# Front of a hybrid attention/recurrence block: the second pair's projection steps set among its transposes, value weights cast earlier, one remainder on GpSimd

## The chip, the cores and the metric

One core of a Trainium2 chip. The metric is the device time of one execution in microseconds; the kernel before takes 1420.89 us in the median of 3 runs (1420.53 to 1420.9). Five engines work beside each other, each with its own queue in a fixed order: PE (TensorE, matrix products into PSUM), DVE (VectorE), ACT (ScalarE), POOL (GpSimd) and SP (SyncE, which issues most transfers).

## The reference, cut to what matters

```
xn = rmsnorm(x, norm1_g)                       # x: 1024 tokens x 1024, fp32
u  = xn @ w_in                                 # all projections
q_sb, k_sb, v_sb, f_raw, i_hg, q_hg, g_hg, gate_sb, gate_hg = split(u)
o_sb = stick_breaking_attention(q_sb, k_sb, v_sb)      # 8 heads of 64
o_hg = hgrn2(...)                                      # 4 heads of 128, gated recurrence
merged = sigmoid(gate_sb) * (o_sb @ w_o_sb) + sigmoid(gate_hg) * (o_hg @ w_o_hg)
h = x + merged @ w_out
h = h + square(relu(rmsnorm(h) @ w_ff1)) @ w_ff2
return rmsnorm(h, final_g)
```

Only the front is touched: the first normalisation, and the projection to the values `v_sb` and to the query and key of head 0.

## The kernel before

Every fp32 operand of a product is written as a rounded high part and a remainder, `h` and `l`. A product `x @ w` is then three matmuls: `xh·wh + xl·wh + xh·wl` (`three`, and `v_part` for the values). The high part is a copy on ACT (`hi_copy`, line 156: a CAST in the profile), the remainder a subtraction on DVE (`lo_sub`, line 161).

The 1024 tokens are 8 blocks of 128, `xt[0..7]`; the profile calls them all x. A block is normalised in this way: half of its squares are summed on ACT, half on DVE (line 281), the two sums are added, GpSimd takes the inverse root (`inv_root`, line 274, the tile n_y), and DVE multiplies the block by it (line 664, the scaling). Blocks 0 and 1 are the first pair, 2 and 3 the second; blocks 4 to 7 follow with their sums wholly on ACT (line 295).

`norm_transpose` turns normalised blocks so that features lie on the partitions: PE transposes 128x128 pieces into a PSUM bank (xnt, line 131), ACT writes the high part xnh (line 348) and DVE the remainder xnl (line 351), which reads the bank and xnh. For a pair there are 8 such banks (one for each of 8 feature slices `kt`), two transposes each. PSUM has 8 banks in all; the running sums of the query/key projection (pjqk) and of two value blocks (two banks pjv) hold three while the second pair is turned.

The value weights come in four tiles, wvr in the profile, split into wvh and wvl (`Unit.split`, the unit is named "wv"). Each tile holds two slices `kt`: tile 0 serves `kt` 0 and 1, tile 1 serves 2 and 3, tile 2 serves 4 and 5 (the third weights) and tile 3 serves 6 and 7 (the fourth).

The first job (`first_job`) is a generator of steps. Each call `st.advance(n, 1)` puts the next `n` steps into PE's queue; their order there is the order of the code. The steps are: four of the query/key projection for the first pair; products of blocks 0 and 1 with the high parts of value tiles 0 and 1; products with their remainders (the last part of these, `kt` 2 and 3, uses the remainder of tile 1); four query/key steps for the second pair; then the value products with tiles 2 and 3, and the rest.

Between `turns["on"] = True` and `False`, ACT and DVE execute their instructions in the order in which the code issues them (`in_turn`). An instruction on GpSimd is not held by that. `owed_wlo` keeps remainders that are to be subtracted later, and `lo_now` issues them.

Of the kernel before, what the change touches and what calls it, by code (L numbers as in the profile page):

```python
# [9 lines left out]
F32 = mybir.dt.float32  # L10
# [4 lines left out]
ALU = mybir.AluOpType  # L15
# [24 lines left out]
def kernel(  # L40
# [19 lines left out]
    nc = tc.nc  # L60
# [14 lines left out]
    def slot(name, dt=F32):  # L75
        return spool.tile([P, 1024], dt, tag="s", name=name)
# [7 lines left out]
    def bank(name):  # L84
        return psum.tile([P, 512], F32, tag="p", name=name)
# [19 lines left out]
    def after(ins, earlier):  # L105
        if earlier is not None and earlier.ins is not ins.ins:
            tc.add_manual_dep(ins.ins, earlier.ins.name, NOSYNC, reason="issue order")
        return ins

    def open_block(name):  # L110
        cur[0] = name
        lane = lanes[name]
        lane.gates = (lane.last,)
        if name == "main":
            lane.ends.append(lane.last)
        else:
            ends = lanes["main"].ends
            lane.gates += tuple(ends[-AHEAD : len(ends) - AHEAD + 1])
# [8 lines left out]
    def matmul(*a, **k):  # L127
        return pe(nc.tensor.matmul(*a, **k))  # L128

    def transpose(dst, src):  # L130
        return pe(nc.tensor.transpose(dst, src, ident))  # L131
# [9 lines left out]
    def lo_now(behind=None):  # L141
        while owed_wlo:
            after(owed_wlo.pop()(), behind)
# [3 lines left out]
    def in_turn(engine, ins):  # L147
        if turns["on"]:
            after(ins, turns[engine])
            turns[engine] = ins  # L150
        return ins
# [3 lines left out]
    def hi_copy(dst, src):  # L155
        hi_last[0] = after(in_turn("act", nc.scalar.copy(dst, src)), hi_behind[0])  # L156

    def lo_sub(dst, src, hi):
        return in_turn(
            "dve",  # L160
            nc.vector.tensor_tensor(out=dst, in0=src, in1=hi.bitcast(F32), op=ALU.subtract),  # L161
        )

    def hi_lo(h, l, src):
        hi_copy(h, src)
        return lo_sub(l, src, h)
# [29 lines left out]
    expo = cpool.tile([P, NT], F32, tag="expo", name="expo")  # L196
# [74 lines left out]

    def inv_root(mean, name):
        y = small.tile([P, 1], F32, tag="rs_y1", name=f"{name}_y", bufs=4)
        nc.gpsimd.tensor_tensor(out=y, in0=mean, in1=expo[:, 0:1], op=ALU.pow)
        return y

    def mean_square(scr, src, before, name):
# [7 lines left out]
        )  # L285
        return out

    last_power = [None]

    last_evac = [None]  # L290

# [27 lines left out]
            c = (kt % 2) * 512 + (tb % 4) * P  # L319
            return h[:, c : c + P], l[:, c : c + P]  # L320

    def norm_transpose(acts, half, b0, n, between=None):

        banks = {}

        def turn_block(kt, b):
            if kt not in banks:
                banks[kt] = bank(f"xnt{half}{kt}_{b0}")[:, 0 : n * P]
            open_block("main")
            transpose(  # L330
                banks[kt][:, b * P : (b + 1) * P],
                xt[4 * half + b0 + b][:, kt * P : (kt + 1) * P],
            )

        ahead = 6 if between else 0
        for kt in range(ahead):
            turn_block(kt, 0)
        if between:
            between()
        for kt in range(KT):  # L340
            hi, lo = acts.t.get((half, kt // 2)) or acts.make(half, kt // 2)
            cs = slice(kt % 2 * 512 + b0 * P, kt % 2 * 512 + (b0 + n) * P)
            for b in range(n):
                if b > 0 or kt >= ahead:
                    turn_block(kt, b)
            pb = banks[kt]
            g = prm[:, G1 + kt : G1 + kt + 1]
            in_turn("act", nc.scalar.activation(hi[:, cs], pb, AF.Identity, scale=g))
            in_turn(
                "dve",  # L350
                nc.vector.scalar_tensor_tensor(
                    out=lo[:, cs],
                    in0=pb,
                    scalar=g,
                    in1=hi[:, cs].bitcast(F32),
                    op0=ALU.mult,
                    op1=ALU.subtract,
                ),
            )

    class Quads:

# [33 lines left out]
        def split(self, i, kp, src, pr=0, n=4):  # L396
            if (i, kp) not in self.hl:
                self.hl[i, kp] = tuple(slot(f"sq{n_}{i}{kp}", F32R) for n_ in "hl")
            h, l = (self.part(t, pr, n) for t in self.hl[i, kp])
            self.last_lo = hi_lo(h, l, self.part(src, pr, n))  # L400
# [44 lines left out]
    class Unit:  # L445
# [28 lines left out]
        def split(self, upto=None):  # L474
            self.load(upto)
            self.hl = self.hl or []
            for i, r in list(enumerate(self.raw))[len(self.hl) : upto]:
                if self.wide:
                    h = slot(f"{self.name}h{i}", F32R)
                    l = slot(f"{self.name}l{i}", F32R)  # L480
                else:
                    h = wpool.tile([P, 1024], F32R, tag="whi", name=f"{self.name}h{i}")
                    l = wpool.tile([P, 1024], F32R, tag="wlo", name=f"{self.name}l{i}")
                self.hl.append((h, l))
                if self.name == "wf1" or self.name == "wv" and i == 1:
                    hi_copy(h, r)
                    owed_wlo.append(lambda h=h, l=l, r=r: lo_sub(l, r, h))
                    continue
                after(after(hi_lo(h, l, r), last_lo[0]), attended[0])

# [73 lines left out]
    st = Stream()  # L564
# [42 lines left out]
    def wide_unit(name, mat, c0, n):  # L607
        rows = 1024 // n * P
        return Unit(
            name,  # L610
            [
                [(0, n, mat[r : r + rows, c0 : c0 + n].rearrange("(k p) c -> p k c", p=P))]
                for r in range(0, D, rows)
            ],
            wide=True,
        )


    xn = Acts("xn")
# [77 lines left out]
    def qk_item(h):  # L697
        u = cols_unit(f"wqk{h}", [(W_IN, C_Q + h * DHS, DHS), (W_IN, C_K + h * DHS, DHS)])
        return f"pjqk{h}", u, qk_epilogue(h)
# [24 lines left out]
    def first_job():  # L724
        name, u_qk, ep = qk_item(0)
        u_qk.__class__ = FirstUnit
        u_v = wide_unit("wv", W_IN, C_V, 512)
        u_v.roomy = range(4)
        open_banks = {}

        def v_part(tb, kt, hi=True, lo=True):
            if kt == 0 and hi:
                open_banks[tb] = bank(f"pjv_{tb}")
            ps = open_banks[tb]
            sh, sl = xn.stat(kt, tb)
            wh, wl = (w[:, kt % 2 * 512 : (kt % 2 + 1) * 512] for w in u_v.hl[kt // 2])
            if hi:
                matmul(ps, sh, wh, start=kt == 0, stop=False)
                matmul(ps, sl, wh, start=False, stop=False)
            if lo:  # L740
                matmul(ps, sh, wl, start=False, stop=kt == KT - 1)

        def v_steps(tb, kts):
            for kt in kts:
                v_part(tb, kt)
                if kt == KT - 1:
                    v_epilogue(open_banks.pop(tb), tb)
                if kt % 2 == 1:
                    yield

        def qk_steps(ps, half, b0, n):
            ts = slice(b0 * P, (b0 + n) * P)
            return proj_half(ps[:, ts], u_qk.hl[0], xn.mov, KT, half, ts=ts)

        def body():
            ps = bank(f"{name}_0")
            yield from qk_steps(ps, 0, 0, 2)
            for hi in (True, False):
                for k0 in (0, 2):
                    for tb in range(2):  # L760
                        for kt in (k0, k0 + 1):
                            v_part(tb, kt, hi, not hi)
                    yield
            yield from qk_steps(ps, 0, 2, 2)
            ep(ps, 0)
            st.prefetch()
            for tb in range(4):
                yield from v_steps(tb, range(4, KT) if tb < 2 else range(KT))
            ps = bank(f"{name}_1")
            yield from qk_steps(ps, 1, 0, 4)  # L770
            ep(ps, 1)
            for tb in range(4, NT):
                yield from v_steps(tb, range(KT))

        return st.add([u_qk], body), u_qk, u_v

    j_first, u_qk0, u_v = first_job()
    j_qk = {0: j_first}

# [1554 lines left out]
    u_v.split(2)  # L2334
    norm1((2, 3), half_means((2, 3)))
    lo_now()
    st.advance(3, 1)
    norm_transpose(xn, 0, 2, 2)
    u_v.split()
    st.advance(5, 1)  # L2340
    norm1(range(4, NT))
    st.advance(8, 1)
    norm_transpose(xn, 1, 0, 4)
# [16 lines left out]
    for i, it in enumerate(items):  # L2360
# [12 lines left out]
        def between():  # L2373
            if before:
                values(*before)

        r = turn(*it, between)
# [135 lines left out]
```

## Time and profile before

| | |
|---|---|
| median of 3 runs | 1420.89 us (1420.53 to 1420.9) |
| the profiled execution | 1421.05 us, span 1419.3 us |
| granted TensorE clock, mean | 0.999 |
| PE busy | 1409.0 us |
| DVE busy | 1087.3 us |
| ACT busy | 684.4 us |
| POOL busy | 147.9 us |

The span is the time from the first to the last instruction in the profile; the execution is some 1.75 us longer. A timeline row has the start and the duration in us, the engine, the line, the operation, the tile written and the tiles read, shapes, and how many alike were put together; in brackets stands how long the engine idled before it and what released it. Instructions of one engine overlap a little in these rows, because the next one starts while the last one drains: the spacing of starts is then the better measure. A matmul row of 0.28 us can stand every 0.12 us.

### The profile page before, as it was taken

The numbers are of one execution on the slowest core, as the hardware profiler recorded it, in microseconds if no ns is written. First come the engines' busy times: TensorE is split into PE (matmuls) and PEld (weight loads), VectorE is DVE, ScalarE is ACT, GpSimd is POOL, SyncE is SP. The second block draws the span as 40 slices with busy tenths as digits, with TensorE's granted clock in tenths as the row PEclk, the third lists the DMA queues.
The fourth block names the chain that finished last, engine by engine and source line by source line (L and its number), as shares of the span: only waits on it lengthen the run. The fifth ranks groups of instructions, "written<-read, shape, count | busy, mean of one in ns | idle before, by whom it ended". The sixth has DMA issues, their size and how long they took to land.

```text
span 1419.3 us, 18799 instructions
## 1 busy us (share of the span) xinstructions
PE 1409.0 (99%) x6848; PEld 1183.7 (83%) x6848; DVE 1087.3 (77%) x1494; ACT 684.4 (48%) x1181; POOL 147.9 (10%) x341
## 2 busy tenths in 40 slices
PE   9999999999999999999999999999999999999997
PEld 8888888888888888888888888888888888888886
DVE  7579988988567888887788897676666657768765
ACT  6356676664243554433344764445444443433343
POOL 3012223210011031000000300000000000000042
PEclk9999999999999999999999999999999999999999
DMA  7024445535135685364585514444446974776825
GB/s 243 26 67 127 106 99 98 107 77 155 60 74 174 221 223 182 123 213 156 163 297 193 185 58 166 163 163 145 140 141 242 355 259 154 275 278 239 275 98 179
DMA packets 163173, 237.72 MB, mean 167 GB/s; under 512 B 26332, under 2 KB 93448, under 8 KB 163080
## 3 DMA queue, kind: packets, MB, share of 16 engines
q1 hardware_dynamic: 146056, 190.37, 40.0%
q0 software_dynamic: 11584, 34.61, 10.0%
q10 hardware_dynamic: 5440, 11.54, 2.3%
q8 instruction: 54, 0.88, 0.2%
q14 instruction: 39, 0.32, 0.1%
HBM read 168.32 MB, written 66.06 MB: 165 GB/s over the span
## 4 chain that ended last, share of the span: by engine, by line
PE 98%; DVE 1%; ACT 1%; POOL 0%; DMA 0%; issue 0%; SPq 0%; DVEq 0%; ACTq 0%
PE pm L128 21%; PE pX L128 9%; PE pW L128 6%; PE pY L128 6%; PE pjqk L128 6%; PE pga L128 4%; PE gX L128 4%; PE gY L128 4%; PE pjf L128 3%; PE pjq L128 3%; PE pys L128 3%; PE pji L128 3%; PE pyh L128 3%; PE pjv L128 3%; PE po L128 3%; PE z L128 2%
## 5 line engine op out<-in xcount | busy, mean ns | idle before, releaser
L156 ACT CAST whid<-w 128x1024 fp32r<-128x1024 f32 x30 | 31.6, 1053 | 154.5 <-PE pm L128 89.8
L826 DVE TENSOR_TENSOR_SCAN rm<-rm,bits 128x511 f32<-128x511 f32 (+7 forms) x72 | 87.3, 1219 | 17.2 <-ACT rm L804 17.1
L128 PE MATMUL pm<-wlod,sh 128*128 128x512 f32 x240 | 93.5, 390 | 0.0
L128 PE MATMUL pm<-whid,sl 128*128 128x512 f32 x240 | 93.4, 389 | 0.0
L128 PE MATMUL pm<-whid,sh 128*128 128x512 f32 x240 | 93.4, 389 | 0.0
L128 PE MATMUL pm<-tl,sh 128*128 128x512 f32 (+1 forms) x210 | 81.3, 387 | 0.0
L128 PE MATMUL pm<-th,sl 128*128 128x512 f32 (+1 forms) x210 | 81.3, 387 | 0.0
L128 PE MATMUL pm<-th,sh 128*128 128x512 f32 (+1 forms) x210 | 81.3, 387 | 0.0
L161 DVE TENSOR_TENSOR wlod<-w,whid 128x1024 fp32r<-128x1024 f32 x30 | 36.7, 1222 | 55.2 <-ACT whid L156 55.1
L161 DVE TENSOR_TENSOR sl<-sa,sh 128x1024 fp32r<-128x1024 f32 x56 | 68.2, 1218 | 0.0
L156 ACT CAST wTh<-pw 128x512 fp32r<-128x512 f32 (+2 forms) x96 | 43.8, 485 | 41.9 <-PE pw L131 41.0
L2141 POOL TENSOR_SCALAR fss<-fss 128x1 f32<-128x1 f32 x8 | 4.5, 561 | 562.0 <-ACT fsc L2136 561.5
L156 ACT CAST sh<-sa 128x1024 fp32r<-128x1024 f32 x56 | 57.2, 1046 | 7.0 <-DMA sa<-ad 7.0
L128 PEld LDWEIGHTS pm<-wlod,sh 128*128 128x128 f32 x240 | 45.0, 187 | 9.9 <-DVE wlod L161 0.4
L128 PEld LDWEIGHTS pm<-whid,sh 128*128 128x128 f32 x240 | 45.1, 188 | 9.4
L161 DVE TENSOR_TENSOR wTl<-pw,wTh 128x512 fp32r<-128x512 f32 (+2 forms) x96 | 49.9, 546 | 3.9 <-ACT wTh L156 3.7
L128 PEld LDWEIGHTS pm<-whid,sl 128*128 128x128 f32 x240 | 45.1, 188 | 9.3
L169 DVE TENSOR_TENSOR bt<-bt,rm 128x511 f32<-128x511 f32 (+7 forms) x72 | 48.9, 684 | 3.5
L804 ACT ACTIVATE rm<-z 128x511 f32<-128x511 f32 (+4 forms) x96 | 48.0, 500 | 5.5 <-PE z L128 2.9
L128 PE MATMUL pX<-sql,t1h 128*128 128x512 f32 x128 | 49.9, 390 | 0.0
L128 PE MATMUL pX<-sqh,t1l 128*128 128x512 f32 x128 | 49.9, 390 | 0.0
L128 PE MATMUL pX<-sqh,t1h 128*128 128x512 f32 x128 | 49.8, 389 | 0.0
(930 smaller groups left out, 4435.9 us busy)
## 6 DMA issues: line engine op xcount, KB each, us to landing
w<-in_w_ff_dram SPq DMA_DIRECT2D x72, 512.0 KB, 4.8
sa<-ad SPq DMA_DIRECT2D x52, 512.0 KB, 6.4
ad<-a SPq DMA_DIRECT2D x32, 256.0 KB, 4.6
ad<-s SPq DMA_DIRECT2D x16, 512.0 KB, 3.3
tw<-in_w_out_dram POOLq DMA_DIRECT2D x24, 256.0 KB, 4.6
pr<-pd SPq DMA_DIRECT2D x10, 512.0 KB, 6.5
x<-in_x_dram SPq DMA_DIRECT2D x8, 512.0 KB, 7.8
xnl<-xnh POOLq DMA_DIRECT2D x8, 512.0 KB, 6.4
```

Of the source, the lines that this page charges most:

```text
L128: return pe(nc.tensor.matmul(*a, **k))
L156: hi_last[0] = after(in_turn("act", nc.scalar.copy(dst, src)), hi_behind[0])
L161: nc.vector.tensor_tensor(out=dst, in0=src, in1=hi.bitcast(F32), op=ALU.subtract),
L169: return nc.vector.tensor_tensor(out=out, in0=a, in1=b, op=ALU.mult)
L804: nc.scalar.activation(rm[:, s0 + c0 - 1 : s0 + m - 1], z[:, c0:m], AF.Sigmoid, scale=-0.125)
L826: sc = nc.vector.tensor_tensor_scan(out=rr, data0=rr, data1=bits[:, 1024 - nk + a : 1024 - nk + b][:, ::-1], initial=rm[:, b : b + 1] if i ...
L2141: nc.gpsimd.tensor_scalar(out=ssq, in0=ssq, scalar1=1.0 / D, scalar2=EPS, op0=ALU.mult, op1=ALU.add)
```

## The change

The projection steps of the second pair are no longer put behind its transposes but among them: `norm_transpose` gets an argument `then`, called after each slice `kt`, and three query/key steps are issued after slices 4, 6 and 7. In the generator, the last part of the remainder products of value tiles 0 and 1 moves behind the four query/key steps of the second pair. The third and fourth value tiles are cast on ACT ahead of the transposes' high parts (`u_v.split()` moves up), the fourth remainder stays on DVE and is owed until after the transposes, and the third remainder is subtracted on GpSimd, issued there behind the latest inverse root (`last_root`).

```diff
     def inv_root(mean, name):
         y = small.tile([P, 1], F32, tag="rs_y1", name=f"{name}_y", bufs=4)
-        nc.gpsimd.tensor_tensor(out=y, in0=mean, in1=expo[:, 0:1], op=ALU.pow)
+        last_root[0] = nc.gpsimd.tensor_tensor(out=y, in0=mean, in1=expo[:, 0:1], op=ALU.pow)
         return y
...
-    last_power = [None]
+    last_power, last_root = [None], [None]
...
-    def norm_transpose(acts, half, b0, n, between=None):
+    def norm_transpose(acts, half, b0, n, between=None, then=None):
...
+            if then:
+                then(kt)
...
-                if self.name == "wf1" or self.name == "wv" and i == 1:
+                if self.name == "wf1" or self.name == "wv" and i in (1, 3):
                     hi_copy(h, r)
                     owed_wlo.append(lambda h=h, l=l, r=r: lo_sub(l, r, h))
                     continue
+                if self.name == "wv" and i == 2:
+                    hi_copy(h, r)
+                    ins = nc.gpsimd.tensor_tensor(
+                        out=l, in0=r, in1=h.bitcast(F32), op=ALU.subtract
+                    )
+                    after(ins, last_root[0])
+                    continue
...
+        def v_quarter(hi, k0):
+            for tb in range(2):
+                for kt in (k0, k0 + 1):
+                    v_part(tb, kt, hi, not hi)
...
-            for hi in (True, False):
-                for k0 in (0, 2):
-                    for tb in range(2):
-                        for kt in (k0, k0 + 1):
-                            v_part(tb, kt, hi, not hi)
-                    yield
+            for hi, k0 in ((True, 0), (True, 2), (False, 0)):
+                v_quarter(hi, k0)
+                yield
             yield from qk_steps(ps, 0, 2, 2)
+            v_quarter(False, 2)
+            yield
             ep(ps, 0)
...
     u_v.split(2)
     norm1((2, 3), half_means((2, 3)))
     lo_now()
+    u_v.split()
     st.advance(3, 1)
-    norm_transpose(xn, 0, 2, 2)
-    u_v.split()
-    st.advance(5, 1)
+    norm_transpose(xn, 0, 2, 2, then=lambda kt: st.advance(1, 1) if kt in (4, 6, 7) else None)
+    lo_now()
+    st.advance(2, 1)
     norm1(range(4, NT))
```

The queues move at three places. PE, at the second pair's transposes, before (xnt is a transpose bank, x_165 and x_169 are token blocks 2 and 3, pjv_316 and pjv_321 the two value banks, wvl_295 the remainder of value tile 1, pjqk the query/key bank):

```order
L131 MATMUL xnt_2_358<-ident,x_165 128x128
L131 MATMUL xnt_2_358<-ident,x_169 128x128
L131 MATMUL xnt_2_363<-ident,x_165 128x128
L131 MATMUL xnt_2_363<-ident,x_169 128x128
L131 MATMUL xnt_2_368<-ident,x_165 128x128
L131 MATMUL xnt_2_368<-ident,x_169 128x128
L128 MATMUL pjv_316<-wvl_295,xnh_237 128x512
L131 MATMUL xnt_2_373<-ident,x_165 128x128
L131 MATMUL xnt_2_373<-ident,x_169 128x128
L128 MATMUL pjv_316<-wvl_295,xnh_237 128x512
L128 MATMUL pjv_321<-wvl_295,xnh_237 128x512 x2
L128 MATMUL pjqk_0_265<-xnh_229,wqk0whi 128x256
```

The same place of PE's queue now, from the fifth pair of transposes on:

```order
L131 MATMUL xnt_2_365<-ident,x_165 128x128
L131 MATMUL xnt_2_365<-ident,x_169 128x128
L128 MATMUL pjqk_0_265<-xnh_229,wqk0whi 128x256
L128 MATMUL pjqk_0_265<-xnl_230,wqk0whi 128x256
L128 MATMUL pjqk_0_265<-xnh_229,wqk0wlo 128x256
L128 MATMUL pjqk_0_265<-xnh_229,wqk0whi 128x256
L131 MATMUL xnt_2_376<-ident,x_165 128x128
L128 MATMUL pjqk_0_265<-xnl_230,wqk0whi 128x256
L128 MATMUL pjqk_0_265<-xnh_229,wqk0wlo 128x256
L131 MATMUL xnt_2_376<-ident,x_169 128x128
L131 MATMUL xnt_2_381<-ident,x_165 128x128
L131 MATMUL xnt_2_381<-ident,x_169 128x128
```

The first query/key products of the pair stand between its fifth and sixth transposes, and the four value products with the remainder of tile 1 have left this place; they now stand behind the last query/key product.

GpSimd, at the inverse roots of the second pair (n_2_y, n_3_y), before:

```order
L274 TENSOR_TENSOR n_2_y<-n_2_ms,expo 128x1
L274 TENSOR_TENSOR n_3_y<-n_3_ms,expo 128x1
L265 TENSOR_SCALAR n_4_ss<-n_4_ss 128x1
L269 TENSOR_TENSOR n_4_y<-n_4_ss,expo 128x1
L265 TENSOR_SCALAR n_5_ss<-n_5_ss 128x1
```

And GpSimd there now (line 493 is the new subtraction):

```order
L274 TENSOR_TENSOR n_2_y<-n_2_ms,expo 128x1
L274 TENSOR_TENSOR n_3_y<-n_3_ms,expo 128x1
L493 TENSOR_TENSOR wvl_317<-wvr_171,wvh_316 128x1024
L265 TENSOR_SCALAR n_4_ss<-n_4_ss 128x1
L269 TENSOR_TENSOR n_4_y<-n_4_ss,expo 128x1
```

The third remainder stands between the root of block 3 and the sums of block 4.

ACT, at the squares of the second pair (n1scr) and its first high parts (xnh), before:

```order
L629 ACTIVATE n1scr_297,n_2_ss<-x_165 128x512
L629 ACTIVATE n1scr_305,n_3_ss<-x_169 128x512
L348 ACTIVATE xnh_229<-xnt_2_338,prm 128x256
L348 ACTIVATE xnh_229<-xnt_2_343,prm 128x256
L348 ACTIVATE xnh_237<-xnt_2_348,prm 128x256
```

And ACT there now:

```order
L638 ACTIVATE n1scr_297,n_2_ss<-x_165 128x512
L638 ACTIVATE n1scr_305,n_3_ss<-x_169 128x512
L156 CAST wvh_316<-wvr_171 128x1024
L156 CAST wvh_320<-wvr_173 128x1024
L348 ACTIVATE xnh_229<-xnt_2_345,prm 128x256
```

The two casts, which stood behind all eight xnh, now stand ahead of the first.

Apart from these places, VectorE has one subtraction less (the third remainder, between the second pair's last xnl and the scaling of block 4), and every engine's queue otherwise holds the same instructions in the same order as before.

## The prediction

> **What bounds the kernel now.** I read the page first, for the engine that carries the chain, then the timelines of PE, DVE, POOL, ACT and SP between 12 and 35 us, where all of the change lies.
>
> ```profile
> PE 1409.0 (99%) x6848; PEld 1183.7 (83%) x6848; DVE 1087.3 (77%) x1494; ACT 684.4 (48%) x1181; POOL 147.9 (10%) x341
> PE 98%; DVE 1%; ACT 1%; POOL 0%; DMA 0%; issue 0%; SPq 0%; DVEq 0%; ACTq 0%
> ```
>
> PE is busy for 99% of the span and is 98% of the chain that ended last. So a change here is worth what it adds to or takes from PE's idle time, and from 23.83 us on, where PE's rows follow each other closely, a shift is passed on to the end. PE in the stage that is rewritten:
>
> ```profile
> 17.68 1.25 PE L131 MATMUL xnt<-ident,x 128*128 128x128 f32 x10
> 19.15 0.83 PE L131 MATMUL xnt<-ident,x 128*128 128x128 f32 x4 [0.21 <-DVE xnl L351]
> 19.73 0.48 PE L128 MATMUL pjv<-wvl,xnh 128*128 128x512 f32 x1
> 20.05 0.38 PE L131 MATMUL xnt<-ident,x 128*128 128x128 f32 x2
> 20.19 0.95 PE L128 MATMUL pjv<-wvl,xnh 128*128 128x512 f32 x3
> 20.97 0.28 PE L128 MATMUL pjqk<-xnh,wqk0whi 128*128 128x256 f32 x1
> ...
> 23.83 0.40 PE L128 MATMUL pjv<-wvh,xnh 128*128 128x512 f32 x1
> ...
> 34.74 3.65 PE L131 MATMUL xnt<-ident,x 128*128 128x128 f32 x32
> 38.15 0.47 PE L128 MATMUL pjv<-wvh,xnh 128*128 128x512 f32 x1
> ```
>
> The stage runs from 17.68 to 23.83, 6.15 us. Its work by start-to-start spacing: a transpose takes 0.107 us (32 from 34.74 to 38.15), a query/key product 0.119 (24 from 20.97 to 23.83), a value product 0.227 (48 from 23.83 to 34.74). So 16 × 0.107 + 24 × 0.119 + 4 × 0.227 = 1.71 + 2.86 + 0.91 = 5.48 us. The other 0.67 us is PE waiting, at the transposes: ten of them fill the free PSUM banks, and each further pair waits for VectorE to empty one (the row at 19.15 names it). That 0.67 us is all there is to win in this stage.
>
> What feeds those transposes:
>
> ```profile
> 14.99 0.94 POOL L274 TENSOR_TENSOR n_y<-n_ms,expo 128x1 f32<-128x1 f32 x1 [7.40 <-DVE n_ms L1284]
> 15.90 0.85 POOL L274 TENSOR_TENSOR n_y<-n_ms,expo 128x1 f32<-128x1 f32 x1
> 15.96 0.76 DVE L664 TENSOR_SCALAR x<-x,n_y 128x1024 f32<-128x1024 f32 x1 [0.17 <-POOL n_y L274]
> 16.79 0.75 DVE L664 TENSOR_SCALAR x<-x,n_y 128x1024 f32<-128x1024 f32 x1
> 17.45 1.22 DVE L161 TENSOR_TENSOR wvl<-wvr,wvh 128x1024 fp32r<-128x1024 f32 x1
> 18.61 3.23 DVE L351 SCALAR_TENSOR_TENSOR xnl<-xnt,prm,xnh 128x256 fp32r<-128x256 f32 x8
> ```
>
> GpSimd's inverse root of token block 3 ends at 16.75 (15.90 + 0.85); 0.04 us later VectorE scales x3 (16.79 to 17.54), then takes the second value remainder, then empties the transposes from 18.61 to 21.84. Every second transpose needs x3. So the x3 scaling is on PE's path with only 0.14 us to spare (17.54 against 17.68).
>
> **PE: the second pair's projection steps among the transposes.** The row at 19.15 is to be filled with products. As the rows of PE's queue with the change show, query/key products now stand between the transposes from the fifth pair on, and the four value products with the second remainder have gone behind all 24 of them. The products wait for the same VectorE rows: the first xnl ends near 19.05 (18.61 plus one of eight, 0.40, and its tail), so PE still stands about 0.3 us there; the last xnl ends at 21.84 plus up to 0.4 if its transpose comes later. With VectorE as before, PE would take 5.48 + about 0.3 = 5.8 us: a gain of 0.3, at most 0.67. I take 0.5 for the sum's good case.
>
> **ACT: third and fourth casts ahead of the transposes' own.**
>
> ```profile
> 14.71 0.24 ACT L629 ACTIVATION_READ_ACCUMULATOR n1scr<-x 128x1 f32 x1
> 18.10 3.03 ACT L348 ACTIVATE xnh<-xnt,prm 128x256 fp32r<-128x256 f32 x8 [3.15 <-PE xnt L131]
> 20.97 2.04 ACT L156 CAST wvh<-wvr 128x1024 fp32r<-128x1024 f32 x2
> ...
> 14.86 1.60 SPq L136 DMA_DIRECT2D prow<-in_lb_logits_dram  x2
> ...
> SPq L136 <- DMA wvr<-in_w_in_dram: 3.4, 4, 1.1
> ```
>
> ACT idles 3.15 us before 18.10; the two casts (2.04) fit from 14.95 on, if their weights are there. SP waited four times for a value transfer (last row: 3.4 us in all), the last two times before the two small loads from 14.86 on, so the third weights had landed by 14.86 and the fourth by 16.46 at the latest: casts end near 15.95 and 17.5, before 18.10. Cost nothing; were the fourth weights 0.7 us late or more, every further us would hold the emptying of the banks.
>
> **GpSimd and VectorE: the third remainder changes engines.** VectorE loses one of its 1.22 us subtractions after the transposes; it is not waited for there (the fourth remainder, at some 22 to 23 us, is needed past 25). So that is worth nothing by itself. What counts is where it goes on GpSimd: right behind the root of block 3 (n_3_y), ahead of the sums of block 4. The 128x1024 subtraction starts the moment the inverse root of x3 ends, which is also the moment VectorE's scaling of x3 is released. How GpSimd and VectorE get on together is in these rows:
>
> ```profile
> 24.15 0.36 POOL L265 TENSOR_SCALAR n_ss<-n_ss 128x1 f32<-128x1 f32 x1 [7.40 <-ACT n1scr L295]
> 25.18 0.75 DVE L664 TENSOR_SCALAR x<-x,n_y 128x1024 f32<-128x1024 f32 x1 [0.72 <-POOL n_y L269]
> 25.23 0.75 POOL L265 TENSOR_SCALAR n_ss<-n_ss 128x1 f32<-128x1 f32 x1
> 26.65 0.79 DVE L664 TENSOR_SCALAR x<-x,n_y 128x1024 f32<-128x1024 f32 x1 [0.72 <-POOL n_y L269]
> 26.70 0.19 POOL L265 TENSOR_SCALAR n_ss<-n_ss 128x1 f32<-128x1 f32 x1
> 26.98 0.86 POOL L269 TENSOR_TENSOR n_y<-n_ss,expo 128x1 f32<-128x1 f32 x1
> ...
> 28.76 0.55 POOL L269 TENSOR_TENSOR n_y<-n_ss,expo 128x1 f32<-128x1 f32 x1
> ...
> 1379.71 4.65 POOL L2145 TENSOR_SCALAR fss<-fss,fss 128x1 f32<-128x1 f32 x1
> ...
> 1383.01 1.22 DVE L161 TENSOR_TENSOR wlod<-w,whid 128x1024 fp32r<-128x1024 f32 x1
> ```
>
> The same one-element operation takes 0.19 us at 26.70 and 0.75 at 25.23, where it ends 0.05 after VectorE's scaling (25.98 against 25.93); the root takes 0.55 alone and 0.86 under a scaling; one took 4.65 and ended at 1384.36, 0.13 after a run of VectorE work with two SBUF inputs ended at 1384.23. So they do not share: one stands until the other has ended, and both the scaling and a subtraction of two SBUF tiles do this to GpSimd. Who comes first: the root at 15.90 began 0.06 ahead of the scaling at 15.96 and ended at 16.75, 0.04 after that scaling (16.71), so its reading was done first and only its writing waited. The subtraction stands exactly where that root stood, right behind a root whose result releases a scaling. I take it to come first.
>
> How long VectorE then stands is not in the trace: GpSimd has no long operation beside a scaling. Bounds: nothing, if the two interleave, up to the whole subtraction. Its length, from the nearest row:
>
> ```profile
> 1410.02 0.74 DVE L2174 SCALAR_TENSOR_TENSOR y<-hb,fr_y,gf 128x512 f32<-128x512 f32 x1
> ...
> 1410.18 1.89 POOL L2151 TENSOR_TENSOR y<-hb,gf 128x256 f32<-128x256 f32 x2 [1.03 <-DVE hb L1284]
> ```
>
> Two 128x256 products ended at 1412.07, and the first could start in earnest at 1410.76: 0.65 each. Four times that is 2.6; with 0.19 of fixed cost in each, 4 × 0.46 + 0.19 = 2.0. I take 2.3. No row has the 1024-wide form; as extremes, VectorE's 1.22 for the same tile below, and four times the longer of the two records, 1.19 (1.89 less the second's 0.7), 4.75 above. GPSIMD Engine Reference, § Performance versus the Vector engine, of the Trainium skill has 4497 ns for an addition of 2048 elements in fp32; half of that, an estimate, is 2.25 us, with which the sum would be the same.
>
> For the bounds of the delay I take the whole length, because all rows above show waiting to the other's end and none shows sharing. The Trainium skill speaks against this change here: SBUF — State Buffer, § Who interferes with whom, says that the two engines share a port pair as an exclusive lock, that whoever starts first keeps it for the whole instruction, and that a two-port scaling, and a subtraction with both inputs in SBUF, are among the operations that ask for it. By that rule VectorE's delay is the whole subtraction, and the trace agrees as far as it goes: 0.75 in place of 0.19, and 4.65. If the two engines did not meet, the sum would be the good case, a gain of 0.5.
>
> **The sum.** The subtraction runs from 16.75 to 19.05; x3 is scaled from 19.05 instead of 16.79, so VectorE's chain moves by 2.26: second remainder from 19.71, xnl from 20.87 to 24.10. PE stands at the second transpose from 17.79 to about 19.85, catches up (ten transposes by 20.9), and then goes at xnl's pace. After the last xnl come two products, 0.24, and the four value products, 0.91: 24.10 + 0.05 + 0.24 + 0.91 = 25.3 against 23.83. Loss 1.5 us. Later work hides nothing of it, PE being the chain; behind the subtraction on GpSimd stand the roots of x4 to x7, wanted first at 24.15, five us after it ends; PE wants x4 to x7 only at 34.74. SP's queue is unchanged. The profiled execution took 1421.05 (span 1419.3 and 1.75 around it) and becomes 1422.55; it lay 0.16 above the median 1420.89, so the median becomes 1422.4.
>
> **The rivals.**
>
> *No delay to VectorE.* VectorE's scaling wins the race at 16.79, or the two interleave, and the subtraction runs under the emptying of the banks, whose first input is PSUM. For it: the start differs by some 0.05 us, and at 25.18 and 25.23 VectorE came first. Against: the row at 15.90. Then the gain of 0.3 to 0.67 is kept: 1420.2 to 1420.6, 1420.4. Chance 0.32.
>
> *GpSimd slips in one place later*, between the scaling (ends 17.54) and the second remainder. VectorE's emptying then starts at 17.54 + 2.3 + 0.04 + 1.16 = 21.04 instead of 18.61, 2.43 later; loss 1.65, 1422.5. It differs from the forecast only in which VectorE row is late, so I count it with it: together 0.56.
>
> *A long subtraction,* slower by over 0.2%. Loss grows one to one with its length, and 2.84 us is reached from 3.65 us on (2.3 + 2.84 - 1.5). At the upper extreme of 4.75 us it is 1.5 + 2.45 = 3.95, 1424.8. For it: the first record of 1.19. Against: part of that was waiting. A falling clock after the pause belongs here too:
>
> ```profile
> 1412.00:1414.00 2.00, 0.16 (x2) 0.00 (x0) 1.32 (x5) 0.78 (x2) 1.65 (x4) 1.00 0.51 191
> 1414.00:1416.00 2.00, 0.00 (x0) 0.00 (x0) 0.88 (x2) 1.35 (x3) 0.01 (x1) 1.00 0.61 223
> 1416.00:1418.00 2.00, 0.00 (x0) 0.00 (x0) 0.00 (x0) 0.00 (x0) 0.00 (x0) 0.83 0.88 301
> ```
>
> After the last matmul (0.16 us of PE after 1412, none after 1414) the granted clock, the last column but two, was still 1.00 up to 1416, so a pause of about 2 us should not lower it. Chance of both 0.10.
>
> The remaining 0.02 is a gain past 0.2% by something unseen.
>
> **How the numbers follow.** About 0.2% (2.84 us) is what a measurement of this kernel can tell from no change. The likeliest case gives 1422.4, with 1422.0 to 1423.0 as its own range (lengths of 2.0 to 2.6, and the later slip). The whole range reaches down over the rival without delay, to 1420.1, and up to 1423.4, short of the long subtraction. Within 0.2% lie the forecast, the later slip and the rival without delay: 0.88. Slower is the long one, 0.10; faster 0.02.
>
> **What would show it.** Right: a POOL row of line 493 starting near 16.75 and some 2.3 long; the x3 scaling on VectorE ending near 19.8 instead of 17.54; a pause of PE of 2 us behind the first transpose; the value products with the third weights starting near 25.3. Wrong: x3 scaled by 17.6 and xnl from 18.6 on with the subtraction beside it, and those value products starting at 23.2 to 23.5; or ACT's xnh rows waiting for the casts, which would put the fault on the weights' landing.

## The result and the profile after

The kernel with the change takes 1422.93 us in the median of 22 runs (1422.45 to 1424.46), the kernel before 1421.05 us in the median of 22 runs beside it (1420.53 to 1421.29). The ratio is 1.0015 with a 95% interval of [1.0009, 1.0021]: slower by 1.9 us, 0.13%, where 1422.4 was forecast. Four of these 22 runs, and four of the 11 of e3 below, took 1424.0 to 1424.6 us at a granted clock of 0.997 or 0.998; they lift e3's median by some 0.3 us, none of them has a trace, and their cause is open. The profiled execution took 1422.93 us, its span is 1421.1 us, and its granted clock is 0.999 as before.

The busy times on the page of the kernel after, to be set beside the same line of the kernel before in the prediction:

```profile
PE 1408.7 (99%) x6848; PEld 1183.2 (83%) x6848; DVE 1088.2 (77%) x1493; ACT 684.7 (48%) x1181; POOL 150.2 (11%) x342
```

PE does the same number of matmuls in nearly the same time (1408.7 us against 1409.0), while the span grew by 1.8 us. So PE waits that much longer. GpSimd has one instruction more and 2.3 us more, VectorE one instruction less and still 0.9 us more, though the subtraction that it lost lasts 1.22. The place is seen in the timeline of the kernel after, here GpSimd and VectorE:

```profile
16.03 0.85 POOL L274 TENSOR_TENSOR n_y<-n_ms,expo 128x1 f32<-128x1 f32 x1
16.54 2.53 POOL L493 TENSOR_TENSOR wvl<-wvr,wvh 128x1024 fp32r<-128x1024 f32 x1
...
16.91 2.71 DVE L673 TENSOR_SCALAR x<-x,n_y 128x1024 f32<-128x1024 f32 x1
19.54 1.21 DVE L161 TENSOR_TENSOR wvl<-wvr,wvh 128x1024 fp32r<-128x1024 f32 x1
20.68 3.03 DVE L351 SCALAR_TENSOR_TENSOR xnl<-xnt,prm,xnh 128x256 fp32r<-128x256 f32 x7
23.99 0.48 DVE L351 SCALAR_TENSOR_TENSOR xnl<-xnt,prm,xnh 128x256 fp32r<-128x256 f32 x1 [0.28 <-ACT xnh L348]
```

The scaling of x3 is the row at 16.91. It lasted 0.75 us before and lasts 2.71 now; it ends at 19.62, 0.55 us after GpSimd's subtraction (16.54 + 2.53 = 19.07). Everything behind it on VectorE moved by about two microseconds. PE in the same timeline:

```profile
17.80 0.27 PE L131 MATMUL xnt<-ident,x 128*128 128x128 f32 x1
19.68 1.20 PE L131 MATMUL xnt<-ident,x 128*128 128x128 f32 x9 [1.60 <-DVE x L673]
20.64 0.36 PE L128 MATMUL pjqk<-xnh,wqk0whi 128*128 128x256 f32 x1
...
23.06 0.38 PE L131 MATMUL xnt<-ident,x 128*128 128x128 f32 x2
...
24.52 0.39 PE L128 MATMUL pjqk<-xnl,wqk0whi 128*128 128x256 f32 x1
24.75 0.28 PE L128 MATMUL pjqk<-xnh,wqk0wlo 128*128 128x256 f32 x1
24.86 1.10 PE L128 MATMUL pjv<-wvl,xnh 128*128 128x512 f32 x4
25.80 0.39 PE L128 MATMUL pjv<-wvh,xnh 128*128 128x512 f32 x1
...
36.69 3.65 PE L131 MATMUL xnt<-ident,x 128*128 128x128 f32 x32
```

One transpose runs, the second stands 1.60 us for the scaled x3. From the first transpose to the first value product with the third weights, which I call the stage from here on, it is 25.80 - 17.80 = 8.00 us, against 6.15 before: 1.85 more. In this execution the stage also begins 0.12 later; the 32 transposes that stood at 34.74 stand at 36.69, 1.95 later. In the medians it is still 1.9: nothing later hides it.

ACT, in the timeline of the kernel after, shows that the two casts cost nothing:

```profile
14.93 1.09 ACT L156 CAST wvh<-wvr 128x1024 fp32r<-128x1024 f32 x1
16.25 1.06 ACT L156 CAST wvh<-wvr 128x1024 fp32r<-128x1024 f32 x1 [0.24 <-DMA wvr<-in_w_in_dram]
20.05 1.93 ACT L348 ACTIVATE xnh<-xnt,prm 128x256 fp32r<-128x256 f32 x5 [2.73 <-PE xnt L131]
...
23.48 0.47 ACT L348 ACTIVATE xnh<-xnt,prm 128x256 fp32r<-128x256 f32 x1 [0.31 <-PE xnt L131]
```

The second cast waited 0.24 us for its weights and ended at 17.31; the first xnh waits 2.73 us for PE, not for a cast, and the last one again for PE. In e1, where PE does not stand for x3, the first xnh still waits 0.84 us for PE, at 18.24, behind casts that ended at 17.39.

### The profile page after: what moved, and what is told of

Same layout as the page of the kernel before. It is cut to its first block, busy times and chain, and to the rows that moved or that the text cites. A ratio compares the mean times of both kernels' runs of the same rounds, so it can differ in the third digit from the quotient of the medians.

```text
span 1421.1 us, 18799 instructions
## 1 busy us (share of the span) xinstructions
PE 1408.7 (99%) x6848; PEld 1183.2 (83%) x6848; DVE 1088.2 (77%) x1493; ACT 684.7 (48%) x1181; POOL 150.2 (11%) x342
## 4 chain that ended last, share of the span: by engine, by line
PE 97%; DVE 1%; ACT 1%; DMA 0%; POOL 0%; issue 0%; SPq 0%; ACTq 0%; DVEq 0%
PE pm L128 21%; PE pX L128 9%; PE pW L128 6%; PE pY L128 6%; PE pjqk L128 6%; PE pga L128 4%; PE gX L128 4%; PE gY L128 4%; PE pjf L128 3%; PE pjq L128 3%; PE pys L128 3%; PE pji L128 3%; PE pyh L128 3%; PE pjv L128 3%; PE po L128 3%; PE z L128 2%
```

## The experiments

The first two rows of the table are those of the result above. Beside e1 to e4 the kernel before took 1421.13 us (33 runs), beside e5 to e8 1421.16 (27 runs), and beside e9 and e10 1421.04 (21 runs); each of the kernels e1 to e10 has 11 runs. Most intervals of the ratio hold 1, so the mechanisms are read from the stage in the traces, and the times stand beside it.

| kernel | what differs | stage, us | time, us | ratio, 95% |
|---|---|---|---|---|
| before | | 6.15 | 1421.05 | |
| after | | 8.00 | 1422.93 | 1.0009 to 1.0021 |
| e1_dve | third remainder on VectorE | 6.05 | 1420.87 | 0.9990 to 1.0008 |
| e2_late | GpSimd's subtraction later, beside xnl | 6.06 | 1421.35 | 0.9993 to 1.0010 |
| e3_extra1024 | before, and an extra subtraction | 8.04 | 1423.28 | 1.0007 to 1.0025 |
| e4_extra512 | the same of half the width | 6.99 | 1421.93 | 0.9997 to 1.0015 |
| e5_lo1behind | second remainder behind xnl | 6.95 | 1422.28 | 0.9998 to 1.0016 |
| e7_x3 | subtraction after the scaling | 6.06 | 1421.43 | 0.9993 to 1.0011 |
| e8_quarters | subtraction in four pieces | 6.88 | 1421.83 | 0.9996 to 1.0013 |
| e9_fill | e1, other products in the gap | 5.59 | 1420.49 | 0.9987 to 1.0005 |
| e10_probe | e1 and one idle tile | 6.06 | 1421.31 | 0.9992 to 1.0011 |

**e1_dve: only the engine of the third remainder undone.** The rest of the change stays.

```diff
+    held_wv2 = []
...
-                    ins = nc.gpsimd.tensor_tensor(
-                        out=l, in0=r, in1=h.bitcast(F32), op=ALU.subtract
-                    )
-                    after(ins, last_root[0])
+                    held_wv2.append(lambda h=h, l=l, r=r: lo_sub(l, r, h))
...
     norm_transpose(xn, 0, 2, 2, then=...)
+    held_wv2.pop()()
     lo_now()
```

> The changed kernel with the third remainder back on VectorE (after the second pair's last xnl, ahead of the fourth remainder); order of PE and ACT as in the change. Theory (GpSimd's subtraction keeps VectorE's scaling of x3 waiting): the scaling of x3 takes 0.75 us again and not 2.7, and the time falls by 1.9 to 2.5 us against the changed kernel, to 0.0 to 0.7 below the kernel before. Rival (the products among the transposes, or the casts ahead of them, cost the time): the time stays 1.5 to 2 us above the kernel before.

Rows of VectorE and PE in the timeline of this kernel:

```profile
17.58 1.22 DVE L162 TENSOR_TENSOR wvl<-wvr,wvh 128x1024 fp32r<-128x1024 f32 x1
18.74 3.04 DVE L352 SCALAR_TENSOR_TENSOR xnl<-xnt,prm,xnh 128x256 fp32r<-128x256 f32 x7
...
17.82 1.14 PE L131 MATMUL xnt<-ident,x 128*128 128x128 f32 x9
...
18.83 0.36 PE L128 MATMUL pjqk<-xnh,wqk0whi 128*128 128x256 f32 x1
19.28 0.39 PE L128 MATMUL pjqk<-xnl,wqk0whi 128*128 128x256 f32 x1
...
23.87 0.39 PE L128 MATMUL pjv<-wvh,xnh 128*128 128x512 f32 x1
```

The whole loss goes with the one subtraction. What the rest of the change brings is 6.15 - 6.05 = 0.10 us of stage; the time is 0.26 us below before, but its interval holds 1, so no gain is shown by the times. Why it is so little is seen in the rows at 18.83 and 19.28: the second query/key product waits for the first xnl, 0.45 us after the first where 0.12 is its spacing. Most of the waiting that the kernel before had at its transposes now stands in front of a product.

**e3_extra1024 and e4_extra512: the subtraction alone, and half of it.** The kernel before with one more subtraction behind the root of block 3, into a tile that nothing reads.

```diff
...
-    norm1((2, 3), half_means((2, 3)))
+    means23 = half_means((2, 3))
+    dummy = slot("dummy", F32R)
+    after(
+        nc.gpsimd.tensor_tensor(
+            out=dummy[:, 0:1024], in0=u_v.raw[1][:, 0:1024],
+            in1=u_v.hl[1][0][:, 0:1024].bitcast(F32), op=ALU.subtract,
+        ),
+        last_root[0],
+    )
+    norm1((2, 3), means23)
```

> The kernel before with one extra 128x1024 subtraction on GpSimd behind the root of x3, into a tile that nobody reads; all else as before. Theory: the scaling of x3 takes about 2.7 us in place of 0.75, everything behind it moves by 1.9 to 2.0, and the time is 1.7 to 2.0 us above the kernel before. Rival (the order or the casts cost the time in the changed kernel): the time is within 0.3 us of the kernel before.

> As the run with the extra subtraction of 128x1024, with 128x512. Theory (VectorE waits for the whole GpSimd instruction, whose length goes with its elements): the subtraction lasts 1.1 to 1.3 us, the scaling of x3 takes 1.5 to 1.8, and the time is 0.7 to 1.0 us above the kernel before. Rival (a fixed cost of meeting, whatever the length): the same loss as with 1024.

GpSimd's subtraction and VectorE's scaling of x3, from the timeline of the kernel with 1024 columns:

```profile
16.44 2.53 POOL L2338 TENSOR_TENSOR dummy<-wvr,wvh 128x1024 fp32r<-128x1024 f32 x1
...
16.81 2.71 DVE L664 TENSOR_SCALAR x<-x,n_y 128x1024 f32<-128x1024 f32 x1
```

And from the timeline of the kernel with 512 (in its code the three 1024 are 512):

```profile
16.53 1.46 POOL L2338 TENSOR_TENSOR dummy<-wvr,wvh 128x512 fp32r<-128x512 f32 x1
...
16.91 1.63 DVE L664 TENSOR_SCALAR x<-x,n_y 128x1024 f32<-128x1024 f32 x1
```

The same two figures, 2.53 and 2.71, come without any other part of the change. Half the width takes 2.53 - 1.46 = 1.07 us off the subtraction and 2.71 - 1.63 = 1.08 off the scaling: VectorE waits microsecond for microsecond. (The subtraction of half the width was expected to take 1.1 to 1.3 us; the scaling lies in the 1.5 to 1.8 expected.) The stage follows with 8.04 - 6.99 = 1.05, and the times with 1.35, of which the intervals leave the size open (e3 is 2.15 above the kernel before, a little over the 1.7 to 2.0 expected). With the order of before, e3 has the same stage as the whole change, 8.04 against 8.00: beside the wait, the new order and the casts won 0.04 us.

**e2_late: the same subtraction, after VectorE's second remainder.** GpSimd first reads one element of that remainder.

```diff
+                    probe = small.tile([P, 1], F32, tag="probe", name="probe")
+                    seen_lo = nc.gpsimd.tensor_scalar(
+                        out=probe, in0=self.hl[1][1][:, 0:1].bitcast(F32), ...
+                    )
+                    after(seen_lo, last_root[0])
...
-                    after(ins, last_root[0])
+                    after(ins, seen_lo)
```

> The changed kernel with the subtraction on GpSimd held back: a one-element GpSimd operation that reads the second value remainder stands ahead of it, so it can start only when VectorE has ended that remainder, near 18.7 us, and runs beside VectorE's emptying of the banks (xnl, whose first input is PSUM). Theory (the two engines wait for each other only where VectorE scales in SBUF or reads two SBUF tiles): xnl keeps its spacing of 0.395 us, and the time is as in the kernel with the remainder on VectorE, 0.0 to 0.7 us below the kernel before. Rival (any VectorE work waits for a long GpSimd one): xnl starts some 2.2 us later, and the time is 1.5 to 2.2 us above the kernel before.

The subtraction and the xnl rows beside it, from the timeline of this kernel:

```profile
18.98 2.39 POOL L499 TENSOR_TENSOR wvl<-wvr,wvh 128x1024 fp32r<-128x1024 f32 x1
...
18.66 3.05 DVE L351 SCALAR_TENSOR_TENSOR xnl<-xnt,prm,xnh 128x256 fp32r<-128x256 f32 x7
```

Seven xnl take 3.05 us beside the subtraction and 3.04 without one (e1), and the stage is 6.06: with one input in PSUM, they did not wait. The subtraction took 2.39 us, and 2.37 where a third of it met no xnl (e5), so it did not wait either. Here neither engine holds the other up, and the gain is still no more than 0.1 us of stage. The time is 0.2 us above the kernel before, where 0.0 to 0.7 below was expected, and 0.5 above that of e1, which the stage does not explain; e10 takes that up.

**e7_x3: the subtraction between the scaling and the second remainder.** GpSimd first reads one element of the scaled x3. This is the later slip of the prediction, brought about.

```diff
+                    seen = nc.gpsimd.tensor_scalar(
+                        out=probe, in0=xt[3][:, 0:1], ...
+                    )
+                    after(seen, last_root[0])
...
-                    after(ins, last_root[0])
+                    after(ins, seen)
```

> The changed kernel with GpSimd's subtraction held until x3 has been scaled, the second remainder still between that and the xnl. Which of the two comes first at the place where my later-slip rival put GpSimd. If VectorE's second remainder (two SBUF inputs) starts first, GpSimd's subtraction stands until it ends: its row starts near 17.8 and lasts 3.2 to 3.6 us, xnl starts near 18.7, and the time is within 0.4 us of the kernel before. If GpSimd slips in, the second remainder lasts some 3.3 us, xnl starts near 20.9 and the time is 1.5 to 2.0 us above the kernel before. Rival (a subtraction with two SBUF inputs does not meet GpSimd): GpSimd's row starts near 17.8 and lasts 2.2 to 2.4, xnl starts near 18.7.

GpSimd's one-element reading and subtraction, and VectorE's second remainder, from the timeline of this kernel:

```profile
17.53 1.09 POOL L494 TENSOR_SCALAR probe<-x 128x1 f32<-128x1 f32 x1 [0.88 <-DVE x L679]
18.59 2.38 POOL L499 TENSOR_TENSOR wvl<-wvr,wvh 128x1024 fp32r<-128x1024 f32 x1
...
17.35 1.22 DVE L161 TENSOR_TENSOR wvl<-wvr,wvh 128x1024 fp32r<-128x1024 f32 x1
```

VectorE's remainder needs nothing new and follows its scaling directly, so it came first, and GpSimd stood: the one element took 1.09 us and ended at 18.62, just behind the remainder's 18.57. The same reading took 0.19 in e2 and e5. The slip did not cost VectorE anything. The subtraction behind the reading, which was expected to stand, took 2.38 beside the xnl. The kernel tests this order with the small reading ahead of the subtraction, not with the subtraction itself at 17.53.

**e5_lo1behind: the scaling free, the second remainder behind xnl.** As e7, and the second remainder moves behind the eight xnl.

```diff
     norm1((2, 3), half_means((2, 3)))
-    lo_now()
     u_v.split()
+    owed_wlo.reverse()
```

> The changed kernel with two edits: GpSimd's subtraction is held until x3 has been scaled (a one-element GpSimd operation that reads x3 stands ahead of it), and the second value remainder, which the change no longer needs early, is subtracted on VectorE behind the second pair's xnl instead of ahead of them. Theory (GpSimd and the emptying of the banks do not meet, and the second remainder's 1.22 us is what keeps PE waiting at its first query/key product with xnl): the first xnl starts near 18.5 instead of 18.7, PE's first value product with the third weights starts at 23.3 to 23.7 instead of 23.87 in the run with the remainder on VectorE, and the time is 0.2 to 0.8 us below the kernel before. Rival (ACT's xnh sets the pace, or the second remainder comes too late for its products): 23.8 or later, time within 0.2 us of the kernel before or above it.

GpSimd, VectorE, ACT and PE in the timeline of this kernel:

```profile
17.87 2.37 POOL L499 TENSOR_TENSOR wvl<-wvr,wvh 128x1024 fp32r<-128x1024 f32 x1
...
18.69 3.04 DVE L351 SCALAR_TENSOR_TENSOR xnl<-xnt,prm,xnh 128x256 fp32r<-128x256 f32 x7 [1.07 <-ACT xnh L348]
...
22.41 2.35 DVE L161 TENSOR_TENSOR wvl<-wvr,wvh 128x1024 fp32r<-128x1024 f32 x2
...
18.18 1.20 ACT L348 ACTIVATE xnh<-xnt,prm 128x256 fp32r<-128x256 f32 x3 [0.95 <-PE xnt L131]
...
23.68 1.20 PE L128 MATMUL pjv<-wvl,xnh 128*128 128x512 f32 x4 [0.63 <-DVE wvl L161]
```

My theory fell. Without the remainder in front of it, xnl still starts at 18.69, because ACT's xnh, which begins at 18.18, sets its pace, and VectorE idled 1.07. The second remainder, now from 22.41 on, came too late, and PE stood for it. What holds is the subtraction's length: 2.37 us, the first 0.8 with VectorE idle and the rest beside xnl.

**e8_quarters: the subtraction in four pieces.** Four instructions of 128x256 at the same place.

```diff
+                    ins = last_root[0]
+                    for c in range(0, 1024, 256):
+                        ins = after(
+                            nc.gpsimd.tensor_tensor(
+                                out=l[:, c : c + 256], in0=r[:, c : c + 256],
+                                in1=h[:, c : c + 256].bitcast(F32), op=ALU.subtract,
+                            ),
+                            ins,
+                        )
```

> The changed kernel with GpSimd's subtraction cut into four of 128x256 at the same place in its queue. Theory (who waits, waits for one instruction, not for the queue): VectorE's scaling of x3 gets in after the first or second quarter and takes 1.3 to 1.9 us in place of 2.7, the second remainder may stand behind a further quarter, and the time is 0.3 to 1.4 us above the kernel before. Rival (GpSimd keeps its place through instructions that follow each other closely): the scaling takes 2.7 us or more again, and the time is 1.7 to 2.3 us above.

The four pieces, and VectorE's scaling and second remainder, from the timeline of this kernel:

```profile
16.59 0.90 POOL L496 TENSOR_TENSOR wvl<-wvr,wvh 128x256 fp32r<-128x256 f32 x1
...
17.45 1.17 POOL L496 TENSOR_TENSOR wvl<-wvr,wvh 128x256 fp32r<-128x256 f32 x1
...
18.58 1.70 POOL L496 TENSOR_TENSOR wvl<-wvr,wvh 128x256 fp32r<-128x256 f32 x1
...
20.25 0.73 POOL L496 TENSOR_TENSOR wvl<-wvr,wvh 128x256 fp32r<-128x256 f32 x1
...
16.96 1.07 DVE L678 TENSOR_SCALAR x<-x,n_y 128x1024 f32<-128x1024 f32 x1
...
17.96 1.74 DVE L161 TENSOR_TENSOR wvl<-wvr,wvh 128x1024 fp32r<-128x1024 f32 x1
```

The ends follow each other in turn: first piece 17.49, scaling 18.03, second piece 18.62, remainder 19.70, third piece 20.28, fourth 20.98. In this run each engine waits for one instruction of the other, not for its queue. So the scaling loses 0.32 us in place of 1.96 (it takes 1.07, less than the 1.3 to 1.9 expected) and the remainder 0.52; the stage gives back 1.12 of the change's 1.85.

Such turns are not the rule everywhere. In the timeline of the kernel before, the one-element operation of GpSimd at 1379.71, shown in the prediction, lasted 4.65 us beside these rows of VectorE, which follow each other without a gap and have two SBUF inputs each:

```profile
1380.14 1.22 DVE L1284 TENSOR_TENSOR w<-w,w 128x1024 f32<-128x1024 f32 x1
1381.27 0.69 DVE L169 TENSOR_TENSOR hb<-hb,gf 128x512 f32<-128x512 f32 x1
1381.88 1.22 DVE L161 TENSOR_TENSOR sl<-sa,sh 128x1024 fp32r<-128x1024 f32 x1
1383.01 1.22 DVE L161 TENSOR_TENSOR wlod<-w,whid 128x1024 fp32r<-128x1024 f32 x1
```

It ended at 1384.36, behind the last of the four. Whether it got no turn between them or needed several is not shown.

By the Trainium skill (SBUF — State Buffer, § Who interferes with whom), the loser of the shared port pair stands for the whole of the other's instruction, two-port scalings and subtractions with both inputs in SBUF among them, while a VectorE instruction with at most one SBUF input, outside the two-port modes, does not contend. The trace agrees in each of these: 2.71 in e3, 1.63 in e4, 1.09 for one element in e7, the turns of e8, and the unchanged 3.05 of e2.

**e9_fill: what the rest of the 0.67 us was waiting for.** From e1, with the four value products of the second remainder in the gap after the fifth pair of transposes, and the query/key steps behind them.

```diff
...
                 v_quarter(hi, k0)
                 yield
-            yield from qk_steps(ps, 0, 2, 2)
             v_quarter(False, 2)
             yield
+            yield from qk_steps(ps, 0, 2, 2)
             ep(ps, 0)
```

> The third remainder on VectorE as in the kernel before, but behind the last xnl; and of the moved steps the four value products with the second remainder stand after the fifth pair of transposes, the query/key steps after the sixth and seventh pair (kt 6 and 7), two of them behind all transposes. Theory 'PE's wait for the first xnl is what is left of the 0.67': those products need the second remainder alone, which is ready at about 18.8, so they cover the 0.45 us from 18.83 to 19.28 that PE waited with the query/key products there. PE then needs 5.48 of work and about 0.1 of waiting from the stage's start: the value products with the third weights start near 23.4 with a stage start at 17.8, a gain of some 0.5 us against before, time 1420.6. Rival 'the pace of the eight xnl sets the end': the last xnl can't end before about 22.3 and two query/key products and nothing else follow it, so PE stands before them and the value products with the third weights start at 23.7 or later, a gain of 0.2 or less.

PE in the timeline of this kernel:

```profile
17.76 1.25 PE L131 MATMUL xnt<-ident,x 128*128 128x128 f32 x10
18.79 1.20 PE L128 MATMUL pjv<-wvl,xnh 128*128 128x512 f32 x4
19.82 0.38 PE L131 MATMUL xnt<-ident,x 128*128 128x128 f32 x2
...
23.35 0.40 PE L128 MATMUL pjv<-wvh,xnh 128*128 128x512 f32 x1
```

The gap is gone, since these products need the remainder that ends at 18.7 and no xnl. The stage is 5.59 us, 0.56 below before and 0.11 above its work of 5.48. The time is 1420.49 us (1420.20 to 1420.82), 0.55 below before and the fastest of all here; the difference in the median is that of the stage, but its interval still holds 1.

**e10_probe: where e2, e5 and e7 lost another 0.4 us.** PE's rows of these three fall behind by 0.3 to 0.5 us between 85 and 820 us, far from the change. Common to them is the one-element tile. From e1, with that tile filled from a constant; nothing waits for it.

```diff
+                    probe = small.tile([P, 1], F32, tag="probe", name="probe")
+                    seen = nc.gpsimd.tensor_scalar(
+                        out=probe, in0=expo[:, 0:1], ...
+                    )
+                    after(seen, last_root[0])
                     held_wv2.append(lambda h=h, l=l, r=r: lo_sub(l, r, h))
```

> As the kernel with the third remainder back on VectorE, with one more tile of one element and a one-element GpSimd operation that fills it from a constant, behind the root of block 3; nothing reads it and nothing waits for it. Theory 'the extra tile or the extra instruction is what makes PE lose 0.4 us between 85 and 600 us in the three kernels that had such a tile': the loss comes again, time about 1421.2 and the shift of PE's rows at 600 us 0.3 to 0.5 above that at 34.7 us. Rival 'it was the late subtraction on GpSimd': no such loss, 1420.9.

The same products of the gated recurrence, much later, in PE's timeline, first of e1:

```profile
815.63 0.50 PE L128 MATMUL pX<-sql,t1h 128*128 128x512 f32 x1
```

And of e10:

```profile
23.88 0.39 PE L128 MATMUL pjv<-wvh,xnh 128*128 128x512 f32 x1
...
816.04 0.50 PE L128 MATMUL pX<-sql,t1h 128*128 128x512 f32 x1
```

At 23.88 against 23.87 the two kernels are even; at 816 us e10 is 0.41 behind, and its time is 0.44 longer; against the runs of before beside each, e1 is 0.26 us below and e10 0.27 above. The traces of all kernels agree: from the 32 transposes near 35 us to these products, PE takes 781.22 to 781.38 us in the four kernels that have the tile (e2, e5, e7, e10) and 780.87 to 780.94 in the seven that do not. So it is the tile or its instruction, not the late subtraction. Which of the two it is, and what it does to PE, is open. The change itself has neither.

## Why the prediction was right

The mechanism came as forecast. The median is 0.5 us above the 1422.4, within the likeliest case's own range of 1422.0 to 1423.0; that it is no further off is in part luck, since a delay taken too long and a tail taken too short partly cancel. By its steps:

- **GpSimd comes first.** The subtraction was to start at 16.75 and take 2.3 us; its row starts at 16.54 and ends at 19.07, and where nothing holds it up it takes 2.37 (e5) to 2.39 (e2). Right. That it would come first was read off one row, with a chance of 0.56 for this and the later slip together.
- **VectorE waits for its whole length.** Shown by e3 and e4: 1.07 us more of subtraction is 1.08 more of scaling. The size was a little off: 2.26 us of delay forecast, 1.96 measured (2.71 - 0.75), since the scaling ends 0.55 after the subtraction, sooner than the 0.75 that it takes alone.
- **The sum: 1.5 lost, 1.85 measured.** This is the step of the forecast that was mis-sized: the time from the first xnl to the third weights' products. xnl began at 20.68, 0.19 sooner than the 20.87 of the sum. I let eight of them follow each other to 24.10, and put two products and the four value products behind that. The last pair of transposes, at 23.06, stands behind the twelve products that the change set among the transposes; so the last xnh came late, at 23.48, the last xnl waited 0.28 for it and ended at 24.47. That is 0.37 of the 0.5 us between 25.3 and 25.80; the products behind it took the rest, 1.33 where 1.20 was put down. So the new order covered next to nothing of the wait: with the order of before and the same wait, e3 has a stage of 8.04 against 8.00.
- **The reorder's good case, 0.3 to 0.67 and taken as 0.5.** Wrong in size: 0.10 (e1). I had seen that PE would stand about 0.3 us before the first xnl product, and it did (0.45 where 0.12 is the spacing), but then took 0.5 all the same, for the rival without delay. With e1's 8.00 - 6.05 = 1.95, the change is 1.95 lost by the subtraction and 0.10 won by the rest. The bound itself, 0.67, was right: e9 wins 0.56 of it with other products in the same gap.
- **Casts on ACT cost nothing.** Right: the weights landed in time for both to end at 17.31. GpSimd's roots of blocks 4 to 7 were covered as well.
- **The rivals.** No delay to VectorE: made in e2, it yields a stage of 6.06, not the 5.5 to 5.85 behind 1420.2 to 1420.6. The later slip: in e7 VectorE came first and lost nothing, so pricing it like the forecast was wrong for a reading that comes 0.18 after VectorE's start. A long subtraction: no, 2.4 us. A falling clock: not in the profiled execution, at 0.999; that a pause of about 2 us leaves the clock alone, as the prediction read off one row, is not shown for the executions without a trace.

## What to carry to other kernels

Moving work to an idle engine is not free when both engines stand for each other's instructions: look what the other engine does in the very stretch, above all when one result releases both. If work must go to GpSimd there, put it beside VectorE instructions that read PSUM (e2), or cut it into pieces, since there the wait was one instruction long (e8). And when products are set into a gap, ask what they wait for: the same gap gave 0.10 us with products that needed the next result, and 0.56 with products that did not (e9).

## What the runs showed of the hardware

- VectorE and GpSimd, meeting in this way with several instructions queued on both, took turns, one instruction each (e8); but a one-element GpSimd operation stood 4.65 us beside four VectorE instructions in a row (kernel before, at 1379.71).
- Where one GpSimd result released both a VectorE scaling and the next GpSimd subtraction, GpSimd came first in all four kernels that have this (after, e3, e4, e8). Behind the root of block 4 in the kernel before it was VectorE, whose row starts at 25.18 against 25.23; what decides is not shown.
- The recorded start of a GpSimd instruction can lie before the end of the one ahead of it: 16.54 against 16.03 + 0.85 = 16.88. The root presumably still waits to write under VectorE's first scaling, which ends at 16.84; then 2.53 in the row is 2.37 to 2.39 of work and some waiting.
- One unread tile of one element and the instruction that fills it go with 0.3 to 0.5 us more, spread over several hundred microseconds that do not use it (e10, and e2, e5 and e7). Differences of that size between kernels with different tiles prove little about the place that was edited.
